# Gate/up projection of an encoder layer: from seven products over two token halves to twenty products over three token thirds

## The chip, the core and the metric

The kernel runs on one core of one Trainium2 chip. The metric is the device time of one execution in microseconds. Before the change the median of three runs is 1613.7 us (1612.8 to 1613.93).

The engines are named as in the profile: PE multiplies matrices (PEld is its weight load), DVE and ACT and POOL work element by element, SP issues loads. All arithmetic is float32. A product is made exact enough by splitting both operands into a high and a low part and adding three matmuls (high x high, high x low, low x high).

## The reference

One encoder layer over 256 prompt tokens and 1024 sample tokens (1280 together, width 1024), attention inside each of the two sequences:

```python
def encoder_layer(x, ...):
    h = rmsnorm(x, attn_norm_g)
    proj = h @ w_in
    a = mla_group(...)          # latent attention, 8 heads
    b = na_group(...)           # 2-D neighbourhood attention, 8 heads
    mix = jnp.concatenate([rmsnorm(a, mla_out_g), rmsnorm(b, na_out_g)], axis=-1)
    x = x + mix @ w_o
    h2 = rmsnorm(x, ffn_norm_g)
    x = x + (jax.nn.silu(h2 @ w_gate) * (h2 @ w_up)) @ w_down     # D_FF = 2816
    return x
```

A final rmsnorm follows. The change concerns `h2 @ w_gate` and `h2 @ w_up`.

## The kernel before

The layer runs in stages: input projection, neighbourhood attention, latent attention, output projection, gate/up projection, down projection. PE goes through them one after the other.

**Output projection and norm.** A loop over ten tiles of 128 tokens (line 1006). For each, 48 matmuls of 512 columns, the residual add (L907), the norm of the sum (L914 to L917), eight transposes (L926), and the eviction of the transposed, normed tokens with their gain by DVE (L929) and ACT (L933) into `R`, where channels lie on partitions. The weights of the first f pair's first products are loaded from tile 6 on.

**Gate/up projection.** The 2816 output columns are taken as 11 pairs of 128 (an f pair). For each f pair there are two projections, gate (i = 0, result G) and up (i = 1, result U). Each is computed as a 2 x 2 x 2 scheme with seven products: two halves of the 1024 channels, two halves of the tokens (640 each), two f blocks. The right operands S[m] are sums and differences of token blocks, split into high and low; they are built once, S1 and S2 in the tile loop, the others (`build_S`) during the first f pair. The left operands are sums of weight blocks: POOL sums (`sum_A`, L980), ACT casts the high part (L969), POOL subtracts for the low part (L970), in a ring of six buffers. `product` runs a product in two token cuts of 320 columns, four chunks of 128 channels each, three matmuls to a chunk. Pairs of products share a PSUM bank (`CHAIN`). After a product its bank is copied by ACT (L1050) or added by DVE (L1052) into the results that need it. For the first f pair gate and up advance together, product by product, since every S is new; afterwards gate runs through all seven products and then up.

`finish` applies silu to gate (ACT, L1067), multiplies (DVE, L1069), forms the sums that the down projection's own seven-product scheme needs (DVE, L1080), and stores seven blocks to `act_d` in DRAM; the stores are issued by ACT, in its queue.

**Order.** A planner sets the order on every engine from simulated times; only SP keeps the order of the program. `tc.issue_after(ins)` holds the block's instructions behind `ins` on its engine. Waits between engines are put in by the framework; each engine works through its queue in order, so an instruction that waits holds up all behind it.

**Down projection.** Seven products over 11 f blocks each, matmuls of 512 columns. `down_first` prepares the first four f blocks during the last projection of gate/up.

## Time and profile before

| | us |
|---|---|
| median of the runs | 1613.7 |
| span of the profiled execution | 1610.3 |
| outside the span (median less span) | 3.4 |
| PE busy | 1582.5 |
| DVE busy | 893.3 |
| ACT busy | 717.2 |
| POOL busy | 666.1 |
| gate/up stage, from the first to the last M matmul | 549.1 |

The profile is of one execution. "M" is the PSUM tile of a gate/up product, "d" that of the down projection, "po" of the output projection, "wc" a weight operand, "S" a token operand, "z" and "zB" the results G and U. A row "x19: 473/491/494" gives the count and the shortest, median and longest duration in ns; a row with a bar gives busy us and mean ns, then the idle time of the engine ahead of it. In brackets after an instruction stand the time that its engine was idle before it and what it waited for. Matmuls overlap their neighbours, so the time of one is read from how many fit into a stretch.

### The profile page before, as it was taken

The page shows a single profiled execution, that of the slowest core. Times are in us where ns is not written, and L with a number is a line of the kernel's source. Part 1 is how long each engine was busy: PE and PEld are TensorE (multiplying, and loading weights), DVE is VectorE, ACT ScalarE, POOL GpSimd, SP SyncE. Part 2 cuts the span into 40 slices and gives each one's busy share as a digit, 9 for nine tenths or more (in the row PEclk, how much of TensorE's full clock was granted, in tenths as well). Part 3 has the DMA queues.
Part 4 walks back from the last instruction along what each step waited for, and adds up shares of the span by engine and source line. Part 5 has one row for each costly group of instructions (what it writes and reads, how often), then busy time and mean ns, then how long its engine had stood idle before and what let it go on. Part 6 is the DMA issues. An engine that isn't in the chain of part 4 may idle for free.

```text
span 1610.3 us, 25767 instructions
## 1 busy us (share of the span) xinstructions
PE 1582.5 (98%) x9616; PEld 1443.1 (90%) x9616; DVE 893.3 (55%) x1501; ACT 717.2 (45%) x1492; POOL 666.1 (41%) x833
## 2 busy tenths in 40 slices
PE   8999999999999999999999999999999999999998
PEld 8998789998888888888899999999999998888886
DVE  5853045566677777443583444334444246886676
ACT  6533144465777777544453323233222332443334
POOL 4633235544211129224676665565666651010002
PEclk9999999999999999999999999999999999999999
DMA  8626022152100030234312232222232237843534
GB/s 294 202 70 160 19 53 63 37 209 62 32 20 26 24 119 20 80 118 144 125 67 65 89 110 97 71 87 89 97 110 76 70 128 269 296 140 96 157 103 155
DMA packets 121772, 171.09 MB, mean 106 GB/s; under 512 B 35376, under 2 KB 65840, under 8 KB 121648
## 3 DMA queue, kind: packets, MB, share of 16 engines
q1 hardware_dynamic: 78880, 120.30, 24.3%
q10 hardware_dynamic: 41952, 46.08, 8.2%
q0 software_dynamic: 816, 3.08, 0.5%
q8 instruction: 75, 1.23, 0.3%
q14 instruction: 49, 0.40, 0.1%
HBM read 118.96 MB, written 50.46 MB: 105 GB/s over the span
## 4 chain that ended last, share of the span: by engine, by line
PE 90%; POOL 3%; ACT 2%; DVE 2%; DMA 1%; issue 1%; SPq 0%; ACTq 0%; POOLq 0%; DVEq 0%
PE M L112 11%; PE M L110 10%; PE M L111 10%; PE d L111 5%; PE d L110 5%; PE d L112 5%; PE o L788 4%; PE tp L778 4%; PE na_o L512 3%; PE po L110 2%; PE pj L110 2%; PE pj L111 2%; PE pj L112 2%; PE po L111 2%; PE po L112 2%; PE S L110 2%
## 5 line engine op out<-in xcount | busy, mean ns | idle before, releaser
L111 PE MATMUL M<-S,wc 128*128 128x320 f32 x1056 | 323.8, 308 | 0.0
L110 PE MATMUL M<-S,wc 128*128 128x320 f32 x1056 | 321.3, 309 | 2.5 <-ACT S L962 1.2
L112 PE MATMUL M<-S,wc 128*128 128x320 f32 x1056 | 312.0, 309 | 2.4 <-POOL wc L970 2.4
L110 PEld LDWEIGHTS M<-S,wc 128*128 128x128 f32 x1056 | 197.3, 188 | 3.7 <-ACT S L962 1.5
L111 PEld LDWEIGHTS M<-S,wc 128*128 128x128 f32 x1056 | 198.2, 188 | 0.0
L112 PEld LDWEIGHTS M<-S,wc 128*128 128x128 f32 x1056 | 194.7, 188 | 3.0 <-POOL wc L970 3.0
L970 POOL TENSOR_TENSOR wc<-A,wc 128x512 fp32r<-128x512 f32 x86 | 121.1, 1409 | 81.6 <-ACT wc L969 81.5
L1052 DVE TENSOR_TENSOR z<-M,z 128x320 f32<-128x320 f32 x120 | 57.2, 487 | 129.6 <-PE M L112 109.1
L969 ACT CAST wc<-A 128x512 fp32r<-128x512 f32 x86 | 53.5, 622 | 158.4 <-PE M L111 148.8
L970 POOL TENSOR_TENSOR wc<-sum,wc 128x512 fp32r<-128x512 f32 x62 | 88.5, 1427 | 85.8 <-ACT wc L969 85.7
L1052 DVE TENSOR_TENSOR zB<-M,zB 128x320 f32<-128x320 f32 x100 | 47.6, 488 | 133.4 <-PE M L112 109.9
L111 PE MATMUL d<-S,S 128*128 128x512 f32 (+1 forms) x314 | 121.1, 386 | 0.0
L112 PE MATMUL d<-S,S 128*128 128x512 f32 (+1 forms) x314 | 120.7, 386 | 0.0
L110 PE MATMUL d<-S,S 128*128 128x512 f32 (+1 forms) x314 | 120.4, 387 | 0.0
L100 DVE TENSOR_TENSOR PT<-tp,PT 128x512 fp32r<-128x512 f32 (+1 forms) x144 | 93.2, 658 | 33.9 <-ACT PT L99 32.7
L969 ACT CAST wc<-sum 128x512 fp32r<-128x512 f32 x62 | 38.4, 619 | 144.0 <-PE M L111 99.6
L99 ACT CAST PT<-tp 128x512 fp32r<-128x512 f32 (+1 forms) x144 | 79.2, 567 | 33.5 <-PE tp L778 30.2
L770 DVE TENSOR_REDUCE mm<-S 128x1 f32<-128x1024 f32 (+1 forms) x80 | 85.0, 1062 | 13.5 <-PE S L112 11.9
L1099 ACT CAST S<-as 128x640 fp32r<-128x640 f32 x58 | 42.2, 728 | 105.7 <-issue 62.7
L772 ACT ACTIVATE ex<-S,mm 128x1024 f32<-128x1024 f32 (+1 forms) x80 | 79.7, 997 | 14.9 <-DVE mm L770 13.6
L801 POOL TENSOR_TENSOR ob<-ob 128x128 f32<-128x128 f32 x40 | 18.5, 461 | 160.8 <-ACT ob L798 157.3
L788 PE MATMUL o<-PT,v 128*128 128x256 f32 x544 | 80.4, 287 | 0.9 <-ACT PT L99 0.9
(432 smaller groups left out, 4115.8 us busy)
## 6 DMA issues: line engine op xcount, KB each, us to landing
as<-act_d SPq DMA_DIRECT2D x73, 320.0 KB
w<-in_w_down_dram SPq DMA_DIRECT2D x44, 256.0 KB
act_d<-z ACTq DMA_DIRECT2D x35, 320.0 KB
act_d<-zB ACTq DMA_DIRECT2D x35, 320.0 KB
A<-in_w_gate_dram SPq DMA_DIRECT2D x42, 256.0 KB
A<-in_w_up_dram SPq DMA_DIRECT2D x42, 256.0 KB
x<-in_x_tm_dram SPq DMA_DIRECT2D x20, 512.0 KB
cT_d<-stg ACTq DMA_DIRECT2D x20, 320.0 KB
```

Of the source, the lines that this page charges most:

```text
L99: i = nc.scalar.copy(out=hi, in_=ps)
L100: nc.vector.tensor_sub(out=lo, in0=ps, in1=hi)
L110: nc.tensor.matmul(out, lhsT=sh, rhs=mh, start=first, stop=False, **kw)
L111: nc.tensor.matmul(out, lhsT=sh, rhs=ml, start=False, stop=False, **kw)
L112: return nc.tensor.matmul(out, lhsT=sl, rhs=mh, start=False, stop=last, **kw).ins
L770: nc.vector.reduce_max(out=nm[:, u:u + 1], in_=S, axis=AX.X, negate=True)
L772: nc.scalar.activation(ex, S, AF.Exp, bias=nm[:, u:u + 1], scale=1.0, accum_out=l[:, u:u + 1])
L778: nc.tensor.transpose(tp[:, j], ex[:, kt * P:(kt + 1) * P], ident)
L788: nc.tensor.matmul(oT, lhsT=vv, rhs=pt[s][g][:, j], start=kt == 0 and s == 0, stop=kt == nkt - 1 and s == 1)
L969: i0 = nc.scalar.copy(out=hi, in_=raw)
L970: i1 = nc.gpsimd.tensor_tensor(out=lo, in0=raw, in1=hi, op=ALU.subtract)
L1052: nc.vector.tensor_add(out=o, in0=ps, in1=a)
```

## The change

Each projection is computed as a scheme of 20 products: four quarters of the channels (256 each), two f blocks, three token thirds of 428, 428 and 424 (the last one padded with zeros to 428). A product has two chunks of 128 channels, three matmuls of 428 columns each. Products are strung into chains: a chain keeps its PSUM bank, and between two products of a chain the partial sum is read out into the results that need it. SEQ gives the order for the ordinary projections; SEQ0 for the first f pair (gate and up together) and for the last projection alone.

The tokens go into X[k, j] (channel quarter k, third j). Sums of the first two thirds, and S of products 9, 13, 17, 3 and 2, are made in the tile loop after tiles 4, 5, 7 and 8; the sums with the last third (`third_2`) are made on DVE right behind the last tile, in two cuts; the other 15 S in the first f pair (`build_S`). The weights come as one load of 1 MB for a projection. In ordinary projections the weight operands are prepared two products at a time in nine jobs (`pairs`), with a ring of four buffers, six of the low parts on POOL and three on DVE; a job is released when the ring's buffer was used for the last time (LAST, `advance`). In the first f pair and in the last projection they are prepared product by product (`operands_of`). Multiplication and sums of the activation run at four places (`activate`), at the end of the last projection all at once. The buffers of `down_first` lie where S of products 9, 13, 17, 3 and 2 and of 15 lay; one of five weight buffers is a new tile.

```diff
-    NS = NQ // 2
+    XC = 428
+    XN = (XC, XC, NTOK - 2 * XC)
...
+    S = {n: (SE[:, i, 0], SE[:, i, 1]) for i, n in enumerate((9, 13, 17, 3, 2))}
+    X = {(k, j): rX.tile([P, 2, XC], F32, name=f"x{k}{j}") for k in range(4) for j in range(3)}
+    X["14"], X["16"] = st[:, 0], st[:, 1]
+    raw = rY.tile([P, 2, 8, 256], F32, name="wraw")
...
+    FIRST = (add_((1, 0), (1, 0), SUB, (0, 0)), put_(3, (1, 0)), add_((2, 0), (3, 0), SUB, (2, 0)),
+             add_((2, 0), (2, 0), ADD, (1, 0)), put_(9, (2, 0)), add_((3, 0), (3, 0), SUB, (0, 0)),
+             put_(2, (3, 0)))
+    SECOND = (put_(13, (0, 1)), add_((2, 1), (3, 1), SUB, (2, 1)), add_((2, 1), (2, 1), SUB, (2, 0)),
+              put_(17, (2, 1)), add_((3, 0), (3, 1), SUB, (3, 0)), add_("14", (2, 1), ADD, (1, 1)),
+              add_((0, 1), (0, 1), SUB, (3, 0)), add_((1, 1), (1, 1), SUB, (3, 0)))
+
+    def third_2(eng, cs):
+        sums(eng, cs, ((1, 0), (1, 2), SUB, (1, 0)), ("16", (2, 1), ADD, (1, 2)),
+             ((2, 0), (1, 2), SUB, (2, 0)), ((2, 0), (2, 0), SUB, (2, 2)),
+             ((2, 2), (2, 2), SUB, "16"), ((1, 2), (3, 2), SUB, (1, 0)),
+             ((3, 1), (2, 0), ADD, (3, 1)),
+             ((3, 2), (2, 0), ADD, (3, 2)))
+
+    def cast_w(hi, lo, raw_, eng=None):
+        i0 = nc.scalar.copy(out=hi, in_=raw_)
+        cast[0] = i0.ins
+        i1 = (eng or nc.gpsimd).tensor_tensor(out=lo, in0=raw_, in1=hi, op=SUB)
...
     for t in range(NT):
...
         if t == 6:
+            for i in range(2):
+                load_raw(0, i)
+            with tc.issue_after(mixed[0]):
+                sum_w(tmp[0], B(2), SUB, B(6))
+                cast_w(ring[0][:, 0], ring[0][:, 1], tmp[0])
         if t == 7:
+            with tc.issue_after(mixed[0]):
+                cast_w(ring[1][:, 0], ring[1][:, 1], B(4))
...
+        for job, ins in zip(LATER.get(t, ()), anchors):
+            with tc.issue_after(ins):
+                job()
+    third_2(dve, slice(0, 296))
+    third_2(dve, slice(296, XC))
...
+    def build_S(n):
...
+        put_S(n, X[RAW[n]], n == 10)
+        if n == 10:
+            sums(nc.vector, FULL, ((0, 0), (0, 0), SUB, (3, 0)), ((0, 0), (0, 0), SUB, (1, 0)))
+        if n == 11:
+            sums(nc.vector, FULL, ((0, 2), (0, 2), SUB, (1, 0)))
+
+    SEQ = ((1, "A", ((0, 2),)), (9, "C", ((1, 0), (1, 2))), (17, "B", ((1, 1),)),
+           (20, "A", ((1, 2),)), (13, "C", ()), (16, "B", ((1, 2),)), (14, "C", ((1, 1),)),
+           (19, "A", ((1, 1),)), (11, "E", ()), (15, "B", ((1, 0),)), (12, "E", ((1, 2),)),
+           (18, "A", ((1, 0),)), (4, "D", ((0, 0),)), (3, "B", ((0, 0),)), (2, "A", ((0, 0),)),
+           (10, "D", ((1, 0),)), (8, "B", ()), (7, "B", ((0, 2),)), (6, "A", ()),
+           (5, "A", ((0, 1),)))
+    SEQ0 = ((9, "C", ((1, 0), (1, 2))), (13, "C", ()), (17, "B", ((1, 1), (1, 2), (1, 0))),
+            (14, "C", ((1, 1),)), (5, "I", ()), (6, "I", ((0, 1),)), (3, "B", ((0, 0), (0, 2))),
+            (18, "A", ((1, 0),)), (2, "A", ((0, 0), (0, 1))), (1, "G", ((0, 2),)), (11, "E", ()),
+            (12, "E", ((1, 2),)), (7, "H", ()), (8, "H", ((0, 2),)), (16, "F", ((1, 2),)),
+            (20, "G", ((1, 2),)), (15, "F", ((1, 0), (0, 0), (0, 2))), (19, "G", ((1, 1), (0, 1))),
+            (4, "G", ((0, 0),)), (10, "G", ((1, 0),)))
...
+    def product(C, chains, written, seq, at, w, bank=None):
+        n, ch, out = seq[at]
+        onto = ch in chains
+        if not onto:
+            chains[ch] = new_bank(bank)
+        ps = chains[ch]
+        h, l = S[n]
+        for kc in range(2):
+            ks = slice(kc * P, (kc + 1) * P)
+            last = mm3(ps, w[0][:, ks], w[1][:, ks], h[:, kc], l[:, kc], kc == 0 and not onto,
+                       kc == 1, onto)
+        for f, j in out:
+            o = C[:, f, j * XC:j * XC + XN[j]]
+            if (f, j) in written:
+                nc.vector.tensor_add(out=o, in0=ps[:, 0:XN[j]], in1=o)
+            else:
+                nc.scalar.copy(out=o, in_=ps[:, 0:XN[j]])
+                written.add((f, j))
...
+    AFTER = {"22": (4,), "12": (7,), "11": (3, 5, 1), "21": (2, 6)}
...
+    def activate(G, U, b, fp):
+        nc.vector.tensor_mul(out=block(U, b), in0=block(U, b), in1=block(G, b))
+        for n in AFTER[b]:
...
             (store_p if fp == NF // 2 - 1 else store)(act_d[n][fp], out)
...
+    NEW_S = (14, 5, 6, 18, 1, 11, 12, 7, 8, 10, 16, 20, 15, 19, 4)
+    AHEAD0 = 2
+    make = operands_of(both, tmp, ring, (14, 5, 6))
...
+    for at in range(20):
+        if at + AHEAD0 < 20:
+            with tc.issue_after(normed[0]) if at else ExitStack():
+                w0.append(make(at + AHEAD0))
+        if at < len(NEW_S):
+            with tc.issue_after(cast[0]):
+                build_S(NEW_S[at])
+        for i, C in enumerate((G, U)):
+            with tc.issue_after(last_mm):
+                mm = product(C, chains[i], written[i], SEQ0, at, (w[:, 0, i], w[:, 1, i]),
+                             0 if at < 3 else None)
...
+            if k == 6:
+                sum_w(pair(4), pair(4), ADD, pair(7))
+                sum_w(T2_[:, 1], T0[:, 0], SUB, pair(4))
+                split(T2_, (4, 10))
+            if k == 7:
+                x = raw[:, i, 0:4].rearrange("p (a b) n -> p b a n", b=2)[:, 1]
+                sum_w(T1, T1, ADD, x)
+                split(T1, (3, 2))
...
+    LAST = (1, 3, 8, 7, 11, 16, 15, 14, 19)
...
+    for n, (fp, i) in enumerate(plan):
+        C = new_C()
...
+        for at in range(20):
...
+            else:
+                advance(20 * n + at)
+                w = state[n][1][seq[at][0]]
+            product(C, chains, written, seq, at, w)
+            if i == 1 and not last_one:
+                if at == 10:
+                    activate(G, C, "22", fp)
+                elif at == 15:
+                    activate(G, C, "12", fp)
+            if i == 0 and at == 15:
+                gate(G, 1)
+            if last_one and at == 9:
+                down_first()
+        if i == 0:
+            gate(G, 0)
         else:
+            for b_ in ("22", "12", "11", "21") if last_one else ("11", "21"):
+                activate(G, C, b_, fp)
```

The other added helpers: `put_S` casts a token operand on ACT and subtracts on DVE for the low part; `operands_of` makes the weight sums of a product on POOL (13 behind the first one) and splits them; `gate` is silu over one f block of all tokens.

461 lines of the change are left out of this document (246 added, 215 removed).

## The prediction

> **What bounds the kernel now.** I read the page first, for the share of each engine.
>
> ```profile
> span 1610.3 us, 25767 instructions
> PE 1582.5 (98%) x9616; PEld 1443.1 (90%) x9616; DVE 893.3 (55%) x1501; ACT 717.2 (45%) x1492; POOL 666.1 (41%) x833
> ```
>
> PE is busy for 98% of the span, so only matmul time or the PE's waits can be saved. The profiled execution has a span of 1610.3 us; the median of the runs is 1613.7 us, so 3.4 us lie outside the span. I work on the span and add these 3.4 at the end.
>
> Next, busy time by stretch: a tile of the out projection, then from the first gate/up matmul to the end of the first f pair, to the start of the last projection, and to its end.
>
> ```profile
> core 0: us, PE busy (x) PEld busy (x) DVE busy (x) ACT busy (x) POOL busy (x), PEclk, DMA share, GB/s
> 777.90:791.00 13.10, 13.10 (x65) 10.41 (x65) 3.98 (x7) 3.10 (x9) 5.83 (x6) 1.00 0.12 43
> 791.20:846.40 55.20, 51.06 (x345) 50.11 (x344) 46.85 (x47) 29.37 (x49) 44.29 (x27) 1.00 0.27 91
> 846.40:1314.80 468.40, 467.99 (x3194) 467.73 (x3193) 196.71 (x274) 136.22 (x248) 288.95 (x211) 1.00 0.27 90
> 1314.90:1340.40 25.50, 25.11 (x170) 24.61 (x169) 14.92 (x23) 10.25 (x19) 10.47 (x9) 1.00 0.33 113
> ```
>
> The change sits in the last three rows, 549.1 us together, and in the tile loop ahead of them. In the long row PE never rests; in the first f pair, DVE (46.85 of 55.20) and POOL (44.29) are nearly full as well. Who made PE wait in 791 to 1341 us, by the waits of PE:
>
> ```profile
> PE M L112 <- POOL wc L970: 2.4, 2, 2.0
> PE M L110 <- ACT S L962: 1.2, 1, 1.2
> PE M L110 <- ACT wc L969: 0.9, 1, 0.9
> PE M L110 <- DVE z L1052: 0.4, 1, 0.4
> ```
>
> That is 4.9 us. Everything else is matmul issue, so the price of one matmul decides. A matmul row's duration overlaps its neighbours, so I divide stretches by counts: M matmuls (320 columns) alone, then the down projection (512 columns).
>
> ```profile
> 846.40:1314.80 468.40, 467.99 (x3194) 467.73 (x3193) 90.47 (x190) 32.03 (x76) 1.00 0.27 90
> ```
> ```profile
> 1400.00:1580.00 180.00, 180.00 (x794) 148.71 (x793) 27.76 (x45) 3.62 (x10) 1.00 0.44 137
> ```
>
> 468.40/3194 = 146.65 ns for 320 columns, 180.00/794 = 226.7 ns for 512: 0.417 ns a column and 13.2 ns fixed. For 428 columns this line gives 146.65 + 108 x 0.417 = 191.7 ns.
>
> **The change, term 1: the matmuls.** Before, a projection of one f pair is 7 products x 2 token cuts x 4 chunks x 3 passes = 168 matmuls of 320 columns: 24.64 us. After, it is 20 products x 2 chunks x 3 passes = 120 of 428: 23.00 us. Over 22 projections, 3696 x 146.65 = 542.0 against 2640 x 191.7 = 506.1: 35.9 us less, of which columns account for 22 and the saved fixed parts for 14.
>
> The Trainium skill, page "TensorE: Matmul & The Clock Gate", section "Back-to-back issue gap", gives N/2.4 + 2.5 ns. By it the two prices would be 135.8 and 180.8 ns, and term 1 only 24.6 us. The trace's 146.65 and 226.7 ns contradict the small fixed part, though not the slope; measurement decides, but other matmuls might pay it differently, so this stays as a rival.
>
> **Term 2: the first f pair.** Prices of the side engines, alone and under load (the two "|" rows are means in 791.2 to 846.4 us):
>
> ```profile
> L970 POOL TENSOR_TENSOR wc<-sum,wc x62: 1286/1297/1872, 828.0 to 1331.0; 128x512 fp32r<-128x512 f32 x62
> ```
> ```profile
> L801 POOL TENSOR_TENSOR ob<-ob x40: 453/459/515, 411.4 to 669.6; 128x128 f32<-128x128 f32 x40
> ```
> ```profile
> L100 DVE TENSOR_TENSOR mT<-trm,mT x20: 680/691/693, 660.0 to 781.4; 128x512 fp32r<-128x512 f32 x20
> ```
> ```profile
> L963 DVE TENSOR_TENSOR zA<-zB,zA x2: 1484/1484/1484, 831.2 to 833.0; 128x1280 fp32r<-128x1280 f32 x2
> ```
> ```profile
> L1052 DVE TENSOR_TENSOR z<-M,z x120: 473/491/494, 811.5 to 1342.3; 128x320 f32<-128x320 f32 x120
> ```
> ```profile
> L963 DVE TENSOR_TENSOR S<-zA,S 128x1280 fp32r<-128x1280 f32 x4 | 7.3, 1828 | 0.0
> ...
> L948 DVE TENSOR_TENSOR zA<-zB,zA 128x512 f32<-128x512 f32 x2 | 3.5, 1788 | 0.0
> ```
>
> DVE pays 0.69 us for 512 and 1.48 for 1280 elements, 1.03 ns an element more; so 856 elements (one token sum or lo part of S) 1.05 us, and a PSUM add of 428 0.49 + 0.11 = 0.60. Work that DVE must finish inside the first f pair: third_2, 8 operations in two cuts (592 elements 0.77, 264 elements 0.43): 9.6; lo parts of 15 new S: 15.7; three sums in build_S: 3.1; three weight lo parts: 2.1; PSUM adds, 18 for each projection by SEQ0, 36 x 0.60 = 21.6; the last tile's residual add, scaling and eviction: 2.2. Sum 54.3 us alone. PE needs 240 x 0.1917 = 46.0 and some 1 us for the last tile's eight transposes. So DVE, not PE, is the bound here: every new S is needed by a product of this same pair, and adds queue behind them.
>
> It will also not be alone. POOL has 13 sums and 15 lo parts, 28 x 1.30 = 36.4 us, and these collide:
>
> ```profile
> 1138.32 1.77 DVE L1069 TENSOR_TENSOR z<-z 128x640 f32<-128x640 f32 x1
> ...
> 1141.85 0.81 DVE L1069 TENSOR_TENSOR z<-z 128x640 f32<-128x640 f32 x1
> ```
> ```profile
> 1138.11 1.30 POOL L970 TENSOR_TENSOR wc<-A,wc 128x512 fp32r<-128x512 f32 x1 [1.00 <-ACT wc L969]
> ```
>
> The same multiplication takes 1.77 us when POOL runs from 1138.11, and 0.81 with POOL idle. PSUM adds never stretch (maximum 0.494). Of DVE's work, 37 operations have two SBUF inputs. Under load the rows show +0.34 us (1.828 against 1.484) to +1.10 (1.788 against 0.691). POOL was busy 44.29/55.20 = 80% there; here it would be some 36.4/67 = 54%. I take +0.35 each, the end nearer to the wide operations: 13 us, so 67 us for the pair. Ends: 55 (no collision) and 54 + 22 = 76 (0.6 each). Before, this pair took 55.2: 12 us given back.
>
> Products 9, 13, 17, 3 and 2 get their S in the tile loop at no cost: the row of a tile has DVE busy 3.98 and ACT 3.10 of 13.10 us, at most four operations of 1.05 us come into one tile, and the out projection's matmuls cover them; POOL loses its differences there.
>
> What is held: build_S sits behind ACT's latest weight cast, so S lo parts on DVE wait for ACT too, and the weight operands sit on POOL behind the last tile's rstd, which they would otherwise delay; both orders only shift work inside the 67 us.
>
> SP is moved past more: at tile 6 it issues two loads of 1 MB ahead of that tile's x, where three of 256 KB stood. From the page's slices:
>
> ```profile
> GB/s 294 202 70 160 19 53 63 37 209 62 32 20 26 24 119 20 80 118 144 125 67 65 89 110 97 71 87 89 97 110 76 70 128 269 296 140 96 157 103 155
> ```
>
> At up to 296 GB/s 2.1 MB take 7 us; x is fetched a tile (13.1 us) before its residual add, so 0, and 7 us at worst.
>
> The Trainium skill, page "SBUF — State Buffer", section "Who interferes with whom", calls the DVE and GpSimd port an exclusive lock; it says of a DVE instruction with two SBUF inputs that it "contends with a GpSimd instruction that reads SBUF". The 1.77 us agree; by full exclusion the pair's two-input work (36.4 + 30.5) would come to 67 us by itself.
>
> **Term 3: the 19 ordinary projections.** ACT's cast is this row (of 846.4 to 1314.8 us):
>
> ```profile
> L969 ACT CAST wc<-A 128x512 fp32r<-128x512 f32 x76 | 47.2, 622 | 148.7 <-PE M L111 144.9 <-DMA A<-in_w_up_dram 2.2 <-PE M L112 1.6
> ```
>
> 19 x 23.00 = 437.0 us of PE. POOL for each: 5 sums and 6 lo parts of 512 at 1.30, 4 sums of 256 at 0.74 (between the 0.459 of 128 and 1.297 of 512): 17.2 us, so POOL alone fits. The tightest operand is that of job 6: its slot is free when product 8 ends, it is needed three products (3.45 us) later, and takes cast 0.62 + lo 1.30; job 7 behind it ends at 3.3 of 4.6. So cover remains, 1 to 1.5 us. What is thin is the accumulation chain: a PSUM bank goes on with the next product of its chain two products (2.3 us) later, and must be read before. At the turn from one f pair to the next, DVE has six multiplications and sums, and ACT's stores wait for them, with the copies of the new pair queued behind. This exists already:
>
> ```profile
> 1147.78 2.16 ACTq L67 DMA_DIRECT2D act_d<-z  x2
> 1149.98 0.43 ACT L1050 COPY zB<-M 128x320 f32<-128x320 f32 x1 [2.82 <-DVE z L1080]
> ```
> There a copy came 2.82 us late and nobody needed it; now up to four copies are needed 2.3 us on. I put 0.8 us on each of 10 turns: 8 us (0 if the order spares the copies, 25 if each turn loses nearly the whole 2.82).
>
> **Term 4: the last projection** runs SEQ0 alone: product 13 goes straight onto the bank that two copies (about 0.5 us each, from 0.42 for 320 columns) must empty, and 2, 4, 10 follow 18, 19, 4 likewise, behind adds of 0.60: 1.3 + 0.9 + 1.5 + 0.9 with a handover each, about 5 us (2 to 9): 28 us. The activations behind it (9 x 0.81) are hidden by the down projection's first four f blocks, 4 x 15 x 0.2267 = 13.6 us. Weight loads keep their bytes; each has more than a projection's time to land. Nothing else moves on SP.
>
> Sum: 67 + 437 + 8 + 28 = 540 us against 549.1: 9 less. 1610.3 - 9 + 3.4 = 1604.7, say 1605 us.
>
> **Rivals.** First, sums behind the last tile stay hidden: the pair at 57, turns 0, the last at 26: 520 us, 1585. For it: PE waited only 4.9 us with DVE 46.85 of 55.20 busy. Against: 54.3 us of DVE work does not fit 47. Chance 0.25.
>
> Second, slower: DVE and POOL's collisions pace every ordinary projection. POOL 17.2, DVE lo parts 3 x 0.69 = 2.1, activation 9 x 0.81 = 7.3 for every second one, 3.65 on average: 22.9 of 23.0 us if they exclude each other entirely (before: 11 x 1.30 + 3.65 = 17.9 of 24.64). With 2 us lost to gaps in each, 19 x 2 less the 8 already counted is 30 more: 1635. It decides from 9/19 = 0.5 us a projection. For it: the 1.77 us row. Against: 4 jobs of lead, and adds that overlap POOL. Chance 0.26.
>
> Third, the 13.2 ns do not go with the number of matmuls: only 52,800 fewer columns x 0.417 = 22.0 us are saved, 14 less, 1619. The rows of 320 and 512 lie on one line, which speaks against it: 0.06. The rule of "TensorE: Matmul & The Clock Gate" above lies near this case.
>
> Waiting can also lower the clock:
>
> ```profile
> 72.05 0.63 PE L233 MATMUL trc<-ident,c 128*128 128x128 f32 x4 [1.95 <-DVE stg L100]
> ```
> ```profile
> 73.50:77.00 3.50, 3.50 (x16) 3.44 (x17) 1.82 (x4) 2.15 (x5) 3.34 (x6) 0.51 0.78 178
> ```
>
> After a wait of 1.95 us in a thinly used stretch PE had half its clock for 3.5 us. In the first pair that costs little, since DVE sets the pace there.
>
> **How the numbers follow.** Forecast case 0.43, its own range 1594 to 1614; the rivals hold 0.25, 0.26 and 0.06. About 0.2% (3.2 us) can be told from no change. Faster: 0.25 and 0.36 of the 0.43, 0.61; same: the 0.07 left and most of the third rival, 0.12; slower: the second rival and a rest, 0.27. The range goes from 1584 (the first rival is 1585) to 1632 (short of the second): the pair's ends 55 and 76, the turns' 0 and 25 and the last projection's 2 and 9 would alone allow 517 to 570 us, and their extremes do not come together.
>
> **What would show it.** M matmuls 191 to 193 ns apart inside a product; the first pair 60 to 75 us with DVE over 85% busy and PE's waits naming DVE S and ACT S, not POOL alone; turns with PE waiting for ACT copies under 1.5 us; the last projection 26 to 31 us. A pitch above 200 ns, or ordinary projections over 23.5 us, would prove me wrong.

## The result and the profile after

The changed kernel takes 1638.26 us (median of four runs, 1636.39 to 1642.2); the kernel before 1613.25 us (median of four). The ratio is 1.0154, with a 95% interval of 1.0138 to 1.0171: 25 us slower. 1605 us had been forecast, with a range of 1584 to 1632, so the forecast had the wrong sign and its range did not hold the time. The profiled execution took 1637.75 us; its span is 1636.0 us.

The head of the page, and then busy time by stretch, as for the kernel before: the first f pair, the first turn (the gate projection behind it), eighteen projections, the last projection, and the rest.

```profile
span 1636.0 us, 23838 instructions
...
PE 1571.9 (96%) x8560; PEld 1399.1 (86%) x8560; DVE 1038.3 (63%) x1646; ACT 773.3 (47%) x1576; POOL 754.0 (46%) x923
```
```profile
793.40:860.20 66.80, 53.64 (x249) 48.50 (x248) 61.37 (x76) 34.32 (x55) 53.50 (x35) 0.90 0.11 40
860.20:889.50 29.30, 25.71 (x122) 23.73 (x122) 23.01 (x25) 10.21 (x16) 26.24 (x19) 0.94 0.31 115
889.50:1331.50 442.00, 425.79 (x2162) 404.36 (x2161) 288.41 (x334) 170.73 (x289) 348.60 (x271) 1.00 0.26 92
1331.50:1363.60 32.10, 26.95 (x121) 22.98 (x120) 22.22 (x37) 14.63 (x32) 16.95 (x21) 0.95 0.23 73
1363.60:1634.00 270.40, 265.02 (x1171) 217.39 (x1170) 190.25 (x283) 107.96 (x183) 21.77 (x31) 0.99 0.52 174
```

PE is busy for 11 us less than before, and the span is 26 us longer: the matmuls got cheaper and the waits ate more than that. The gate/up stage takes 570.2 us where it took 549.1 and where 540 were forecast. DVE went from 893 to 1038 us.

An up projection runs without a stall:

```profile
938.66:962.04 23.38, 23.38 (x121) 22.51 (x120) 12.84 (x16) 9.55 (x16) 18.52 (x15) 1.00 0.19 66
```

120 matmuls in 23.38 us: 194.8 ns each, where 191.7 had been forecast. The starts of the M matmuls give the time of each projection: the first f pair 66.86, the first gate behind it 29.25; then the up projections take 23.37 to 23.40 and eight of the nine further gate projections 25.76 to 25.83 (the ninth 25.24); the last projection, from its first matmul's start to its last one's, 31.95. So the first turn from one f pair to the next costs 5.9 us and each later one about 2.4. PE's waits in the long row, in all, how often, and the longest:

```profile
PE M L110 <- ACT wr L991: 9.8, 9, 1.2
PE M L110 <- ACT C L1113: 6.4, 9, 0.8
```

Two waits at each of nine turns, both for ACT. Here is one turn (its gate projection begins at 962.04), first ACT with its queue for DMAs, then DVE. The bracket tells how long ACT had stood idle, and behind what:

```profile
967.72 0.33 ACTq L67 DMA_DIRECT2D act_d<-C  x1
968.14 0.62 ACT L991 CAST wr<-wt 128x512 fp32r<-128x512 f32 x1 [1.88 <-DVE C L1138]
...
969.01 0.33 ACTq L67 DMA_DIRECT2D act_d<-C  x1
969.38 0.51 ACT L1113 COPY C<-M 128x424 f32<-128x424 f32 x1 [0.20 <-issue]
970.82 2.16 ACTq L67 DMA_DIRECT2D act_d<-C  x2
973.02 0.62 ACT L991 CAST wr<-wraw 128x512 fp32r<-128x512 f32 x1 [3.13 <-DVE C L1138]
```
```profile
963.17 2.69 DVE L1132 TENSOR_TENSOR C<-C 128x640 f32<-128x640 f32 x2
965.78 6.84 DVE L1138 TENSOR_TENSOR C<-C 128x640 f32<-128x640 f32 x4
972.54 0.58 DVE L1111 TENSOR_TENSOR C<-M,C 128x424 f32<-128x424 f32 x1
```

DVE works six two-input operations off in a row, 9.5 us: the first takes 0.84 us, the sums of L1138 1.7 us each with POOL at work, where an operation of this shape took 0.81 with POOL idle. The stores on ACT wait for these sums, and a cast that the weights need waits behind the stores for 1.88 and 3.13 us. PE then waits 0.71 us for a PSUM copy and 1.15 us for a weight cast:

```profile
969.94 0.46 PE L110 MATMUL M<-SE,wr 128*128 128x428 f32 x1 [0.71 <-ACT C L1113]
973.69 0.46 PE L110 MATMUL M<-x,wr 128*128 128x428 f32 x1 [1.15 <-ACT wr L991]
```

In the first f pair the longest wait is for the low part of S14, which DVE makes only at 809.71, behind the first cut of the last third's sums, three low parts of weights, four PSUM adds and three of the second cut's eight sums:

```profile
PE M L111 <- DVE s L959: 4.8, 1, 4.8
PE M L112 <- POOL wr L993: 2.8, 2, 1.5
PE M L110 <- ACT s L958: 2.0, 1, 2.0
PE M L110 <- ACT x L958: 1.4, 1, 1.4
```

### The profile page after: what moved, and what is told of

It is laid out like the page before. It is cut to its first block, busy times and chain, and to the rows that moved or that the text cites. A ratio compares the mean times of both kernels' runs of the same rounds, so it can differ in the third digit from the quotient of the medians.

```text
span 1636.0 us, 23838 instructions
## 1 busy us (share of the span) xinstructions
PE 1571.9 (96%) x8560; PEld 1399.1 (86%) x8560; DVE 1038.3 (63%) x1646; ACT 773.3 (47%) x1576; POOL 754.0 (46%) x923
## 4 chain that ended last, share of the span: by engine, by line
PE 80%; DVE 10%; ACT 3%; DMA 2%; issue 2%; POOL 2%; SPq 0%; ACTq 0%; POOLq 0%; DVEq 0%
PE M L110 8%; PE M L111 8%; PE M L112 8%; PE d L110 5%; PE d L112 5%; PE d L111 5%; DVE C L1138 4%; PE o L788 4%; PE tp L778 4%; PE na_o L512 3%; PE pj L110 2%; PE pj L111 2%; PE pj L112 2%; PE po L110 2%; PE po L112 2%
## 5 line engine op out<-in xcount | busy, mean ns | idle before, releaser
L1111 DVE TENSOR_TENSOR C<-M,C 128x428 f32<-128x428 f32 (+1 forms) x263 | 154.2, 596 | 151.3 <-issue 77.2
L993 POOL TENSOR_TENSOR wr<-wt,wr 128x512 fp32r<-128x512 f32 (+1 forms) x113 | 156.7, 1387 | 108.2 <-ACT wr L991 108.1
L991 ACT CAST wr<-wt 128x512 fp32r<-128x512 f32 (+1 forms) x113 | 67.6, 600 | 161.2 <-PE M L111 124.5
L111 PE MATMUL M<-s,wr 128*128 128x428 f32 x352 | 127.2, 362 | 4.8 <-DVE s L959 4.8
L110 PE MATMUL M<-s,wr 128*128 128x428 f32 x352 | 127.3, 362 | 3.6 <-ACT s L958 2.0
L112 PE MATMUL M<-s,wr 128*128 128x428 f32 x352 | 126.7, 361 | 3.0 <-POOL wr L993 3.0
L110 PE MATMUL M<-x,wr 128*128 128x428 f32 x264 | 95.8, 363 | 13.6 <-ACT wr L991 10.9
L1113 ACT COPY C<-M 128x428 f32<-128x428 f32 (+1 forms) x132 | 66.0, 513 | 86.5 <-PE M L112 84.6
L112 PE MATMUL M<-x,wr 128*128 128x428 f32 x264 | 91.1, 359 | 1.4 <-POOL wr L993 1.4
L110 PE MATMUL d<-SE 128*128 128x512 f32 (+1 forms) x238 | 92.1, 388 | 0.0
L991 ACT CAST wr<-wraw 128x512 fp32r<-128x512 f32 (+1 forms) x94 | 55.4, 599 | 77.6 <-PE M L111 47.1
L111 PE MATMUL d<-SE 128*128 128x512 f32 (+1 forms) x238 | 92.0, 387 | 0.0
L112 PE MATMUL d<-SE 128*128 128x512 f32 (+1 forms) x238 | 91.7, 388 | 0.0
L801 POOL TENSOR_TENSOR ob<-ob 128x128 f32<-128x128 f32 x40 | 18.5, 464 | 156.2 <-ACT ob L798 141.1
L110 PE MATMUL M<-SE,wr 128*128 128x428 f32 x220 | 80.5, 366 | 8.9 <-ACT C L1113 7.5
L1138 DVE TENSOR_TENSOR C<-C 128x640 f32<-128x640 f32 x55 | 86.2, 1599 | 0.4
```

What stands on the lines that cost most here:

```text
L110: nc.tensor.matmul(out, lhsT=sh, rhs=mh, start=first, stop=False, **kw)
L111: nc.tensor.matmul(out, lhsT=sh, rhs=ml, start=False, stop=False, **kw)
L112: return nc.tensor.matmul(out, lhsT=sl, rhs=mh, start=False, stop=last, **kw).ins
L991: i0 = nc.scalar.copy(out=hi, in_=raw_)
L993: i1 = (eng or nc.gpsimd).tensor_tensor(out=lo, in0=raw_, in1=hi, op=SUB)
L1111: nc.vector.tensor_add(out=o, in0=ps[:, 0:XN[j]], in1=o)
```

## Experiments

Where a projection's or a product's time is given without a row, it is the distance between the starts of its first matmul and the next one's; the last projection's ends at the start of its last matmul. Products are counted from the first (1) to the twentieth (20) here; "behind product 2" in an edit is the loop's own count from 0.

### The turns

**Stores on another queue.**

```
-            (store_p if fp == NF // 2 - 1 else store)(act_d[n][fp], out)
+            (store_p if fp == NF // 2 - 1 else load)(act_d[n][fp], out)
```

> Only change: the ordinary f pairs' activation stores are issued on SP instead of ACT. Theory A (at a turn ACT's queue stands still behind stores that wait for DVE's activation sums, and the PSUM copies and weight casts behind them come late): the gate projections at a turn fall from 25.8 us to 23.4 to 23.9 us, ten of them, 19 to 24 us in all, about 1615 us; PE's waits for ACT's casts (10.9 us) and ACT's PSUM copies (7.5 us) nearly vanish. Theory B (DVE itself is late there, because its 1.6 us operations collide with GpSimd, and PSUM adds and casts would wait whoever issues the stores): turns keep 25 us or more, 1630 us or more, and PE's waits change their name to DVE.

1647.14 us, ratio 1.0214 [1.0198, 1.0229]. Two things happened. The gate projections fell to 24.9 us, 0.9 of the 2.4, and PE's waits changed their name to DVE:

```profile
PE M L110 <- DVE C L1111: 10.8, 9, 1.3
```

So both theories were half right: the stores held ACT, and behind that DVE's row of sums holds a PSUM add for 1.2 us. The time rose because the first f pair's seven stores now stood on SP ahead of the next pair's weight loads, which SP reached at 870.33 (in the changed kernel it issues them at 847.57):

```profile
863.57 6.66 SPq L64 DMA_DIRECT2D act_d<-C  x7
870.33 0.74 SPq L64 DMA_DIRECT2D wraw<-in_w_gate_dram  x1
```
```profile
PE M L110 <- ACT wr L991: 20.6, 1, 20.6
```

PE stood still for 20.6 us, and the first pair with what follows took 87.4 us. Later runs leave the first pair's stores on ACT.

**The row of sums spread out.**

```
+            if pending and i == 0 and at >= 2 and at % 2 == 0:
+                with tc.issue_after(add[0]):      # add[0]: the PSUM add issued last
+                    pending.pop(0)()              # one multiplication, sum or store
...
-                activate(G, C, b_, fp)
+                pending.extend(act_steps(G, C, b_, fp))
```

> Only change: the two multiplications and four sums that an ordinary f pair still owes at its end are no longer issued in a row at the turn, but one behind every second product of the next gate projection (products 2 to 12), each behind the PSUM add issued last; their stores stay on ACT. Theory A (the row of sums on DVE, 1.6 us each beside GpSimd, holds the PSUM adds, and the stores that wait for it hold ACT): the nine later gate projections fall from 25.8 us to 23.4 to 23.8, about 20 us in all, near 1618 us. Theory B (the amount of DVE and GpSimd work beside each other, not its being in a row, makes the waits): gate projections keep 25 us or more, as the same work only moves, 1632 us or more.

1624.53 us, ratio 1.0071 [1.0054, 1.0087]: 13.7 us less than the changed kernel. (The steps are seven, one of them a store alone, so they reach to product 14 of the loop's count.) Eight of the nine later gates fell to 24.13 to 24.21. That is theory A in kind, two thirds of it in size: the row is what costs. The ninth, with the same order, took 23.38, no more than an up projection; POOL, which has no ordinary projection to prepare weights for behind it, is busy 16.54 us there instead of 21.41. In the next runs the gates named are these eight, where nothing else is said.

**The first turn spread as well, and the stores on SP.**

```
-    for b_ in ("22", "12", "11", "21"):
+    for b_ in ("22", "12"):
         activate(G, U, b_, 0)
+    for b_ in ("11", "21"):
+        pending.extend(act_steps(G, U, b_, 0))
...
+            (store_p if fp == NF // 2 - 1 else load if fp else store)(act_d[n][fp], out)
```

> As the run that spreads the sums, with two more edits: the first f pair's own late sums are spread likewise, and the stores of all later ordinary f pairs are issued on SP. Theory A: the first gate projection behind the first f pair falls from 29.3 us to 24 to 27, the other gates to 23.4 to 23.5, 1611 to 1616 us. Theory B (the stores do not matter once the sums are spread): as the run with the sums spread, apart from the first turn.

1621.54 us, ratio 1.0059 [1.0044, 1.0074]. The first turn fell from 29.25 to 27.26; the other gates stayed at 24.14 to 24.19. Once the sums are spread, the queue of the stores does not matter (theory B).

**GpSimd's sums cut short.** Every sum of weights writes 16 columns only; POOL's low parts remain.

```
+        ix = (slice(None),) * (len(o.shape) - 1) + (slice(0, 16),)
+        (eng or nc.gpsimd).tensor_tensor(out=o[ix], in0=a[ix], in1=b[ix], op=op)
```

> Every sum of weights for the gate/up projections, nearly all on GpSimd, is cut to 16 columns, so the weight operands are not the reference's; GpSimd loses some 9 of the 19 us it is busy in an ordinary projection, and DVE keeps all its work. Theory A (collisions with GpSimd make DVE late: 37 x 0.35 us in the first pair, and 1.6 for 0.81 us in the sums of a turn): the first pair falls from 66.9 to 58 to 62 us, gate projections at a turn from 25.8 to 24.2 to 25, DVE's sums of activations to 1.1 to 1.3 us. Theory B (DVE's own amount and order of work): the pair 65 us or more, gates 25.5 or more.

1605.35 us in one run. Every later gate projection ran in 23.36 to 23.39 us, the first turn in 23.33, and the first f pair in 58.6 us. The long stretch (seventeen projections) and the first pair:

```profile
900.20:1297.50 397.30, 397.30 (x2041) 383.27 (x2040) 237.08 (x318) 160.28 (x273) 192.99 (x257) 1.00 0.27 98
```
```profile
794.90:853.40 58.50, 52.42 (x249) 47.32 (x248) 54.58 (x78) 34.20 (x55) 33.86 (x39) 0.94 0.12 46
```

The same four sums of one turn took 4.27 us here, and 6.84 above:

```profile
950.41 4.27 DVE L1142 TENSOR_TENSOR C<-C 128x640 f32<-128x640 f32 x4
```

So with less of GpSimd's work beside it DVE is through with the row in time, though nothing was reordered. Cutting GpSimd's sums also shortens GpSimd's own path to the weight operands; the run does not part the two in the first pair. At the turns that path is not what PE waited for: the cast that ended its 1.15 us, at 973.02 above, reads loaded weights (wr<-wraw) and no sum of GpSimd's.

**Earlier spreading.** All three edits together: steps spread, stores on SP, and the late splits of the last projection (below); the seven steps behind products 2, 3, 5, 6, 7, 9, 10, or 0, 1, 2, 4, 6, 8, 10.

```
-            if pending and i == 0 and at >= 2 and at % 2 == 0:
+            if pending and i == 0 and at in (2, 3, 5, 6, 7, 9, 10):
```

> Three edits together: late activation steps spread over products 2, 3, 5, 6, 7, 9 and 10 of the next gate projection, first turn included; stores of later ordinary f pairs on SP; the down projection's first splits behind the PSUM adds of the last three products. Theory A (the 0.8 us that the spread gates still lose in products 12 to 16 come from sums running beside weight lo parts there, and go when the sums end before): gates 23.4 to 23.6, the last projection 29, 1609 to 1613 us, level with the kernel before. Theory B (denser sums hold the adds of products 3 to 10 instead): gates 24.2 or more, 1617 us or more.

> As the run with all three edits, but the late activation steps stand behind products 0, 1, 2, 4, 6, 8 and 10. Theory A: gates 23.4 to 23.6, 1609 to 1613 us. Theory B: the first steps, in a row again, hold the PSUM copies and adds of products 2 to 5, gates 24 or more, 1616 us or more.

1621.28 us, ratio 1.0042 [1.003, 1.0055], with gates of 24.09 to 24.14, and 1625.79 us, ratio 1.0076 [1.0062, 1.009], with gates of 24.65 to 24.70. Neither kept what theory A said; the earlier positions were worse. In the first of the two, DVE had nothing running for 5 us early in the gate projection that began at 1055.64, since a sum that is held behind a PSUM add waits for that add's matmuls:

```profile
1056.71 0.90 DVE L1134 TENSOR_TENSOR C<-C 128x640 f32<-128x640 f32 x1
1062.94 0.60 DVE L1112 TENSOR_TENSOR C<-M,C 128x424 f32<-128x424 f32 x1 [5.32 <-PE M L112]
```

**Half of the row at once.** So four of the seven steps were put back into that gap, and three behind products 2, 4 and 6 (stores on SP, first turn spread, late splits as above; at the first turn all seven steps go behind products 2, 4, 6, 7, 8, 9 and 10).

```
+                    while len(pending) > 3:
+                        pending.pop(0)()
...
+            if pending and i == 0 and at in (2, 4, 6, 7, 8, 9, 10):
```

> All three edits of the combined run, but of the seven late activation steps of an ordinary f pair (two multiplications, four sums, five stores) the first four are issued at once at the turn, where DVE stood idle for some 4 us ahead of the first PSUM add, and the last three behind products 2, 4 and 6 of the next gate projection. Theory A (the rest of the loss comes from steps that run too late): gates fall from 24.1 to 23.4 to 23.7, 1613 to 1617 us. Theory B (GpSimd and DVE share the time, whatever the order): gates stay at 24.0 or more, 1620 us or more.

1615.4 us, ratio 1.0016 [1.0007, 1.0025]. All nine later gate projections took 23.38 to 23.43 us: these turns cost nothing. The view of PE's waits names none from 915 to 1312 us, and PE rests for nothing:

```profile
915.20:1312.90 397.70, 397.70 (x2041) 382.63 (x2040) 274.38 (x319) 160.32 (x273) 340.97 (x256) 1.00 0.27 98
```

DVE's sums are still stretched; one PSUM add now stands in the middle of them:

```profile
965.73 3.21 DVE L1141 TENSOR_TENSOR C<-C 128x640 f32<-128x640 f32 x2
969.28 0.60 DVE L1112 TENSOR_TENSOR C<-M,C 128x424 f32<-128x424 f32 x1 [0.34 <-issue]
969.80 0.98 DVE L1141 TENSOR_TENSOR C<-C 128x640 f32<-128x640 f32 x1
```

POOL is busy 20.1 us a projection here (340.97/17), and was 19.4 without the reordering (348.60/18). So the collision with GpSimd makes the row long, but it is the row's place that makes PE wait: at the nine later turns either taking most of the collisions away or moving the row (with the stores on SP) is enough. The first turn took 31.3 us in this profile, of a run of 1618.1 us where the median is 1615.4, and 27.1 us in the profile of the version with the second cut later (below), whose order at that turn is the same: one profile does not fix it.

**The remaining three later.** As above, behind products 6, 7 and 8 (and the first turn's seven steps behind 6 to 12; that turn took 31.1 us, as before).

> As the run with half of the steps at once, but the last three stand behind products 6, 7 and 8. Theory A (too late is what costs): gates of 23.9 to 24.3, worse than with products 2, 4 and 6. Theory B: no difference of over 0.1 us.

1627.94 us, ratio 1.0093 [1.008, 1.0107], gates 24.64 to 24.69 (the ninth still 23.38): 1.3 us a turn for a shift of four products or less. Theory A held in direction, and the loss was larger than expected.

### The first f pair

**The last third's sums later.**

```
-    third_2(dve, slice(0, 296))
-    third_2(dve, slice(296, XC))
...
+        if at == 1:
+            with tc.issue_after(low[0]):      # behind the low part of S5
+                third_2(dve, slice(0, 296))
+                third_2(dve, slice(296, XC))
```

> Only change: the last third's sums (both cuts) are issued in the first f pair behind the S of product 5 instead of at once behind the last tile. Theory A (the pair is bound by how much DVE has to do, 61.4 us busy of 66.8): the waits of products 1 to 4 move to later products, the pair takes 62 to 67 us, the time falls by 0 to 5 us. Theory B (the order is what costs: the sums run ahead of the last tile's scaling and of the S of product 14, both needed at once): the pair takes 55 to 59 us, about 9 us less, near 1629 us.

1643.78 us, ratio 1.0196 [1.0179, 1.0213]; the pair grew to 72.2 us. Both theories failed: the move cost 5.3 us. The long waits have other names:

```profile
PE M L110 <- DVE C L1110: 8.0, 2, 7.2
PE M L111 <- DVE s L959: 7.5, 2, 5.8
```

The sums now ran as a block ahead of PSUM adds, and PE waited 7.2 us for one add. In this pair, where DVE is busy for nine tenths of the time, what stood behind the block paid for it in both places.

**Seven of the sums left out.**

```
-    third_2(dve, slice(0, 296))
-    third_2(dve, slice(296, XC))
+    sums(dve, FULL, ("16", (2, 1), ADD, (1, 2)))
```

> Leaves out seven of the eight sums of the last third, 8.4 us of DVE's work by the prediction's prices, so the values of that third are not the reference's. Theory A (the first f pair takes as long as DVE works in it): the pair falls from 66.9 to 57 to 60 us. Theory B (it is the order of the work at its start): the 13 us lost in products 1 to 3 go, and the later waits stay, 54 to 57 us. Theory C (weight operands on GpSimd pace it): it stays over 63 us.

1634.79 us in one run; the pair took 62.0 us, 4.8 less for some 8.4 us of DVE's work:

```profile
794.20:856.20 62.00, 52.36 (x249) 47.63 (x248) 56.86 (x62) 34.24 (x55) 52.88 (x35) 0.94 0.11 43
```

That lies between theories A and C. DVE's busy time fell by 4.5 us only (61.37 to 56.86), in part because some of the sums had run before the pair began, and the pair fell by as much. So where the work itself was changed, the pair followed DVE's busy time: 61.4 of 66.8 us, 56.9 of 62.0, 54.6 of 58.5 with GpSimd's sums cut. It does not follow it closely: among runs whose pair took 66.0 to 66.8 us DVE was busy for 60.8 to 63.7, and the move above, with all the work kept, gave 72.2.

**The second cut alone later**, behind the low part of S14 (on top of the half row).

```
-    third_2(dve, slice(296, XC))
...
+        if at == 0:
+            with tc.issue_after(low[0]):
+                third_2(dve, slice(296, XC))
```

> As the run before in this call, and the second cut of the last third's sums (132 columns, 3.4 us of DVE) is issued behind the low part of the S of product 14 instead of ahead of it. Theory A (that cut's place makes the first long wait, 4.8 us for DVE's low part): that wait falls to 1 to 2 us and the first pair from 66.8 to 62 to 64 us. Theory B (DVE has to work it off anyway before product 9): the wait goes to a later product, the pair stays at 66 us or more.

1615.02 us, ratio 1.0012 [1.0003, 1.002]. The pair took 66.02 us against 66.05 in the run beside it: theory B. The wait for S14's low part fell from 5.2 to 4.2 us and two waits for PSUM adds rose from 1.9 to 4.2 us in all. Only three of the cut's eight sums, some 1.3 us, had stood ahead of that low part.

### The last projection

**The down projection's first splits behind the last weight cast.**

```
-            split_f(a_ring[f], z[:, f])
-            split_f(w_ring[f], rw_)
+            early.append((f, z[:, f], rw_))
...
+            if last_one and at == 16:
+                with tc.issue_after(cast[0]):
+                    down_split()
```

> Only change: in the last projection the splits of the down projection's first four operands are issued at the end of the products, behind ACT's last weight cast, instead of in the middle; their loads stay. Theory A (products 13 to 18 of the last projection wait for ACT, which works off the down projection's casts ahead of the weight casts): the projection falls from 32.0 to 27 to 29 us, the time by 3 to 5 us. Theory B (the chains of SEQ0, each product straight onto the bank that a drain must empty, make the waits): the projection keeps 31 us or more, and the down projection may start later by up to 3 us.

1637.59 us, ratio 1.0156 [1.0141, 1.0171], as without the edit; the projection took 32.2 us. Yet much moved: products 14 to 17, which had taken 2.15, 2.64, 2.46 and 1.73 us, ran in 1.17 each, as theory A says, and products 18 and 19 rose from 3.55 and 2.84 to 4.76 and 5.35. They wait for PSUM adds:

```profile
1355.08 0.73 PE L110 MATMUL M<-x,wr 128*128 128x428 f32 x1 [3.43 <-DVE C L1111]
...
1360.43 0.70 PE L110 MATMUL M<-s,wr 128*128 128x428 f32 x1 [2.84 <-DVE C L1111]
```

The splits that no longer held ACT now stood ahead of these adds on DVE. One wait took the place of another. Part of the lost time is the clock, which was granted at half from 1354.05 on, for 10.24 us:

```profile
1354.05:1364.29 10.24, 6.37 (x16) 5.28 (x17) 10.17 (x16) 1.41 (x3) 2.81 (x5) 0.50 0.47 171
```

The twelve matmuls of the last two products stand 0.36 us apart there instead of 0.195, about 2 us. Without the edit half the clock was granted for 3.4 us:

```profile
1350.99:1354.40 3.41, 3.41 (x9) 2.73 (x10) 3.07 (x5) 0.41 (x1) 3.15 (x3) 0.50 0.01 2
```

**The splits behind the last PSUM adds**, one behind those of each of the last products, two behind the last.

```
+            if last_one and at in (17, 18, 19):
+                down_split(2 if at == 19 else 1)      # issue_after(add[0])
```

> Only change: in the last projection the down projection's first four operands are split one behind the PSUM adds of product 17, one behind those of 18 and two behind those of 19, so no split stands ahead of a weight cast on ACT or of these adds on DVE. Theory A (splits and activations that are queued ahead of the PSUM adds of 17 and 18 make the last two products wait, as products 18 and 19 took 4.8 and 5.4 us when the splits were held behind the last weight cast only): the projection falls from 32.0 to 27 to 29 us, and the down projection's start loses up to 1.5 of it; 1633 to 1636 us. Theory B (the chain onto the same bank itself): 31 us or more remain.

1636.88 us, ratio 1.0148 [1.0133, 1.0163]. The projection fell to 28.9 us (theory A), and the rest of the span grew from 272.6 to 274.0 us, so 1.4 of the 3.0 us are given back behind it.

### The price of a matmul

**Other column counts in the same matmuls.** The middle four of a product's six matmuls on fewer columns:

```
+    SIZE = (428, 424, 416, 400, 384, 428)
```

> Of the six matmuls of each product the middle four run on the first 424, 416, 400 and 384 columns instead of 428, so part of the sums is left out; only the distance from one matmul's start to the next is to be read, size by size. Theory A (a line: 0.417 ns a column, and a fixed part that is 13.2 ns at 320 and 512 columns but 16.6 ns in this stage): 193.3, 190.0, 183.3 and 176.6 ns. Theory B (428 is a bad size, and the others lie on the old line of 13.2 ns): 189.9, 186.5, 179.9 and 173.2 ns, with 195 left at 428.

```
+    SIZE = (428, 320, 352, 320, 384, 428)
+    OFF = {(0, False): 0, (0, True): 8, (1, False): 4, (1, True): 12}      # S 5, 18, 10, 16
```

> The middle four matmuls of each product run on 320, 352, 320 and 384 columns, so part of the sums is left out; in the products of S 5, 18, 10 and 16 their token columns begin 4, 8 or 12 columns later, at multiples of 64 bytes within the tile, elsewhere at column 0. Only the distances from start to start are to be read. Theory A (the price grows faster than the line above 320 columns, whatever the tile): 146.7 at 320, about 161 at 352, 175 at 384. Theory B (the tiles of this kernel, 1712 bytes a row, cost 1.5 to 3 ns wherever a read begins off a multiple of 64 bytes): 148 to 150 at 320, and 146.7 in the four shifted products.

1626.01 and 1598.56 us, one run each. Median distance from start to start, in ns, over the projections from 890 us on, and the line of the prediction beside it:

| columns | 320 | 352 | 384 | 400 | 416 | 424 | 428 |
|---|---|---|---|---|---|---|---|
| measured | 146 | 161 | 175 | 182 | 189 | 193 | 195 |
| 13.2 + 0.417 N | 146.6 | 160.0 | 173.3 | 180.0 | 186.7 | 190.0 | 191.7 |

Between 320 and 428 columns a column costs 0.45 ns, not 0.417. At 320 columns it made hardly a difference where the columns began (146 ns shifted, 147 not), so it is not the tiles' rows of 1712 bytes (theory A of the second run; of the first run neither, since the slope differs, not the fixed part).

The steeper line does not end at 428. In the profile of the kernel before, the input projection's matmuls of 512 columns ("pj") stand 233 ns apart; the first and the last of a stretch of 34:

```profile
206.23 0.39 PE L112 MATMUL pj<-hT_h,wqk_l 128*128 128x512 f32 x1
...
213.92 0.39 PE L112 MATMUL pj<-hT_h,wqk_l 128*128 128x512 f32 x1
```

That is 7.69 us for 33 distances, and 146 + 192 x 0.45 = 232 ns. In the output projection the median is 231 ns. So it is the down projection with its 226.7 ns that lies off this line. Why the same size costs 227 ns in one place and 233 in another stays open.

### The first turn, and all edits together

**The first turn's late steps as at the others**, then **the first split behind product 18 and three behind 19**, then the second cut put back:

```
+    while len(pending) > 3:
+        pending.pop(0)()
```

> As the version with the second cut moved; in addition the first f pair's late steps are treated like all others: four at once at the turn, three behind products 2, 4 and 6. Theory A (the first turn is a turn like the others): it falls from 27.1 us to 23.5 to 25, 1611 to 1613 us. Theory B (GpSimd's weights for the next f pair, which start only here, or the PSUM copies, set it): 26 us or more.

> As the run before in this call, but the down projection's first split stands behind product 18 and the other three behind product 19. Theory A (the split ahead of the PSUM adds of product 18 makes products 17 and 18 late): the last projection falls from 29.5 us to 27 to 28, and the down projection loses less than 1 us at its start. Theory B (the chain onto the same bank): 29 us or more, or the gain is lost at the down projection's start.

> As the run with the late split, but the second cut of the last third's sums is back at its place behind the last tile. If that cut's place matters: the first pair stays at 66 to 67 us here and is 1 us or more shorter in the other two; if not, all three agree within 0.5 us in the first pair.

| | us | ratio | first pair | first turn | last projection |
|---|---|---|---|---|---|
| first turn | 1614.06 | 1.0006 [0.9997, 1.0014] | 66.1 | 28.0 | 29.5 |
| and split late | 1613.97 | 1.0005 [0.9996, 1.0014] | 66.1 | 28.0 | 28.1 |
| and second cut back | 1617.79 | 1.0021 [1.0012, 1.0029] | 66.7 | 27.9 | 28.3 |

The first turn did not follow the rule (theory B); in the first of these runs its PE waits 2.8 us for PSUM adds and 2.2 us for weights from POOL and DVE. The late split brought the last projection to 28.1 us, just short of theory A's 27 to 28, and the time did not change. The run with the second cut back scatters from 1613 to 1620 us and its profile is of the 1613.15, so what its median lost is not seen there; its first pair, 0.7 us longer, lies between the two readings. The best version is level with the kernel before:

```profile
792.20:858.30 66.10, 51.57 (x249) 46.44 (x248) 63.70 (x77) 34.29 (x55) 54.79 (x36) 0.95 0.11 40
858.30:886.33 28.03, 24.68 (x121) 22.15 (x120) 22.95 (x24) 10.20 (x16) 24.64 (x18) 1.00 0.33 120
886.33:1307.40 421.07, 421.07 (x2161) 405.19 (x2160) 287.27 (x334) 169.86 (x289) 359.41 (x271) 1.00 0.27 97
1307.40:1335.70 28.30, 25.37 (x121) 22.64 (x121) 16.08 (x30) 14.66 (x32) 13.91 (x19) 0.97 0.16 57
1335.70:1610.50 274.80, 266.72 (x1172) 217.89 (x1170) 194.81 (x291) 108.18 (x183) 22.49 (x32) 0.99 0.52 174
```

Its gate/up stage takes 543.5 us, 5.6 less than before the change, and the stage behind it 274.8 instead of 270: the gain is given back there, half of it as in the changed kernel without edits (272.4).

## Why the prediction was wrong

**What bounds the kernel** was read rightly: nearly nothing but matmul issue before. **Term 1** had the right sign and was too large. 194.8 ns instead of 191.7 makes 120 x 22 x 3.1 ns = 8 us; the saving is 542.0 - 2640 x 0.1948 = 27.7 us, not 35.9. The step that failed is the line through two points, 320 and 512 columns, used for a size between them: the measured sizes lie above it. Its second point, the down projection, was a cheap place for 512 columns; with the 233 ns of the input projection, in the same profile, the line gives 146.65 + 108 x 0.450 = 195.2 ns for 428. The formula that the Trainium skill gives on its page "TensorE: Matmul & The Clock Gate", section "Back-to-back issue gap", makes an estimate of 180.8 ns, lower still than the measured 194.8. The page gives that formula for a single matmul by itself, which the prediction did not say.

**Term 2** came out in its number: 67 us forecast, 66.86 measured. That is in part luck. DVE's busy time was 61.37 us against 54.3 alone and 13 of collisions in the sum, so the sum holds some 6 us too much for collisions; DVE then stood idle for 5.4 us, which the sum has at nothing. POOL was busy for 53.50 of 66.80 us, 80%, where 54% had been assumed. The mechanism, DVE as the bound, is borne out by the runs with less work above. As the prediction had said, PE's waits name S parts from DVE (4.8 us) and ACT (2.0 and 1.4 us), and not POOL alone (2.8 us).

Two costs ahead of the pair were put at nothing and were not: from its first matmul to the first M matmul the output projection's stage takes 133.3 us, 2.1 more than before. The sums in the tile loop, put at no cost, stand ahead of the split of a normed tile, and PE waited 0.8 us for that at 726.8 and 728.5. The two loads that SP issues ahead of a tile's x, put at 0 and at worst 7 us, cost 1.2 us, on a way that was not thought of. A weight cast stood on ACT ahead of the split of a normed tile and waited for the second load; DVE and PE waited behind it:

```profile
752.56 0.62 ACT L991 CAST wr<-wraw 128x512 fp32r<-128x512 f32 x1 [5.30 <-DMA wraw<-in_w_up_dram]
753.08 0.58 ACT L99 CAST mT<-trm 128x512 fp32r<-128x512 f32 x1
```
```profile
PE trm L893 <- DVE mT L100: 1.7, 2, 1.2
```

The longer of these two waits is the one behind the load. This is read from the trace; no run tried it.

**Term 3** is where the prediction failed. It named the place and the mechanism, the turn with ACT's stores ahead of copies, and gave it 0.8 us; 2.4 us was measured at the nine later turns (2.38 to 2.45, the last 1.86) and 5.9 at the first, 27 us in all instead of 8. The term was mis-sized because the row of DVE's operations was given no length: the 0.8 us were set between 0 and the 2.82 us by which a copy came late before. Alone the six would take 6 x 0.81 = 4.9 us. With POOL at work all but the first took 1.4 to 1.9 us, so the row lasts 9.5 us, over eight products, and not one wait but two come of it: ACT's queue (0.9 us of the 2.4, by the run with the stores on SP) and DVE's own PSUM adds. The prediction had the price in hand, the multiplication of 1.77 us beside POOL, and used it for the first pair alone. Its upper end, 25 us, was near. A projection over 23.5 us had been named as a sign of being wrong; the gates took 25.8. At the first turn PE waited 3.0 us for a low part from POOL and 0.6 us for DVE, and half the clock was granted for 3.4 us from 866.29 on, some 1.7 us by estimate; its spreading brought 2 us of the 5.9.

The second rival, collisions that pace every ordinary projection, had the right cause and the wrong form; that its 1635 us lie near the measured 1638 is luck. The up projections run in 23.38 us without a stall, with POOL busy 18.5 of them; only the turns lose, and with the sums in another order the nine later turns lose nothing with the same collisions. Nor was the first rival near, whose sums stay hidden, or the third: 320 columns cost 146 ns in this kernel too. The third rival's time was also put in the wrong place: 1619 us is 5 us more than before, beyond the 3.2 us that the prediction can tell apart, and yet most of it was counted as no change.

The Trainium skill's page "SBUF — State Buffer", section "Who interferes with whom", states an exclusive lock, and that a DVE instruction with at most one SBUF input, outside its two-port modes, does not contend with GpSimd. The traces agree as far as they go: two-input operations were stretched (0.81 to 1.7 us), while PSUM adds, with one SBUF input, kept 0.60. Whether the lock is exclusive no run here shows.

**Term 4** was 28 us and is 31.95. The chains were counted; not counted was that the down projection's splits stand ahead of weight casts on ACT and of PSUM adds on DVE. Without both, 28.1 to 28.9 us remain, the forecast value. Of the 4 us too few, some 1.7 are the half clock of 3.4 us (an estimate from the row above), which in the runs with the later splits falls at the projection's end and behind it.

The sum closes: against 540 us the stage lost 7.2 by the matmuls of 19 ordinary projections (0.38 us each), 19 by the turns and 4 by the last projection, 570 in all. Outside the stage 2.2 us were lost ahead of it and 2.5 behind, where 180 us hold 787 matmuls instead of 794,

```profile
1420.00:1600.00 180.00, 180.00 (x787) 147.40 (x786) 129.02 (x194) 69.94 (x117) 8.28 (x9) 1.00 0.43 132
```

so 228.7 ns for the same 512 columns, 2.3 us over 1170 of them. By the starts in the trace, the 222 matmuls whose operands lie in `st` and `SE` stand 233 ns apart, 1.4 of these 2.3 us; most others keep 227. Why that pair of buffers costs more is open.

The range missed, too: the ends that the prediction itself gave to its terms reach 570 us, which is what the stage took, but its range stopped at 1632 us because "their extremes do not come together", and the matmul price and the rest of the span had no ends at all.

## What to carry to other kernels

Where a change makes PE's stage shorter, price the side engines' longest uninterrupted row at its durations under load, and compare it with the time until the next thing behind it on the same queue is needed: here 9.5 us of sums stood against 2.3 us of slack. Averages of busy time did not show it; 65% of DVE in the long stretch (288.41 of 442.00) was enough to lose 2.4 us at every later turn. A store that waited for DVE carried its wait into the queue that issued it: 1.88 and 3.13 us of ACT at a turn, and 20.6 us of PE once behind SP. Moving the stores, the last third's sums or the splits moved the wait, and only the trace of that run told to whom; one order of the row, of the five tried, removed it at the later turns. And a price between two known sizes is taken from all the places that show such sizes, not from one.

## What the runs showed of the hardware that was not expected

- A matmul's price between 320 and 428 columns rises by 0.45 ns a column (146 to 195 ns), while 320 columns and the 512 of the down projection together give 0.417. With the 233 ns of 512 columns in the input projection it is again 0.45.
- The down projection's 512-column matmuls took 226.7 ns in one kernel and 228.7 in the other, at a granted clock of 1.00 in both stretches; in the changed kernel those with one pair of buffers took 233 and most others 227.
- In the first f pair the granted clock was 0.90 on average: half the clock for 10.2 us from 804.85 on and for 3.4 us from 828.75 on. The first of these began as a wait of PE of 2.03 us ended. What it cost in this pair no run tells.
